# First-layer attention with key blocks 0-127, 128-255 and 256-271: the two 16x16 corners of four heads in one masked product

## The chip, the cores and the metric

One core of one Trainium2 chip runs the whole forward pass. The metric is the device time of one execution in microseconds (us).

## The reference

A two-layer decoder trunk in fp32: 16 meta tokens are put in front of 256 tokens (272 in all), model width 2048, 16 heads of 128, feed-forward width 8192. The first layer uses forgetting attention, the second stick-breaking attention; each is followed by a squared-ReLU MLP. The change touches the first layer's attention only:

```python
def forgetting_attention(q, k, v, cum_logf):
    for qs, qe in query_blocks(q.shape[1]):        # (0,16), (16,144), (144,272)
        s = jnp.einsum('bqhd,bkhd->bhqk', q[:, qs:qe], k[:, :qe]) * scale
        s = s + cum_logf[:, :, qs:qe, None] - cum_logf[:, :, None, :qe]
        s = jnp.where(k_pos[None, :] <= q_pos[:, None], s, -jnp.inf)
        p = jax.nn.softmax(s, axis=-1)
        outs.append(jnp.einsum('bhqk,bkhd->bqhd', p, v[:, :qe]))
```

So the queries 16-143 see the keys 0-143, and the queries 144-271 see the keys 0-271, each with the causal mask.

## The kernel before, in words

Activations lie feature-major: the 2048 features are 16 chunks of 128 partitions, with the tokens along the row. Every general product runs in `gemm_group`: 512 output features, 16 chunks of the contraction, four accumulators. Weights come by DMA as `raw` tiles; ScalarE rounds them to `whi` (line 197), VectorE puts the rest into `wlo` (line 198), and three products per chunk and output block (lines 220 to 222) give nearly fp32 precision. `raw`, `whi` and `wlo` each rotate through three buffers.

The first layer's attention runs over four groups of four heads. In a group the query, key and value projections are three calls of `gemm_group`, and the attention's own steps are spread between them:

- Scores: two products per head (line 365), for 128 queries against 144 keys and for 128 queries against 272 keys, in full fp32. The probabilities of a head lie in one tile `s` with 144 + 272 = 416 columns, queries on partitions. The 16 meta queries of the four heads go through one packed 64-row product (line 378) into `s0`.
- Transposes: to multiply by the values, the probabilities are turned with the keys on partitions. Per head that is three 128x128 transposes (lines 396 to 398) into `pp`, copied to `pp_sb`. The kernel before takes the key blocks as 0-15, 16-143, 144-271; the three transposes cover the last two.
- The meta block, keys 0-15: `packed` (line 316, on GpSimd) gathers 32 columns of each of the four heads into one 128-column tile `pk_sm`, once for each query block. Lines 403 to 405 transpose the two tiles and `s0` into `pm`, and ScalarE copies all of it to `pm_sb` (line 407).
- Values: after the value projection, `packed` gathers the first 32 values of the four heads (`pk_vm`); they are transposed (line 413), copied to `vm_sb` by ScalarE (line 415) and used at once for the meta queries (`pom`, line 419). GpSimd then copies the 16 meta rows of each head into its own slab of `vz` (line 417), a tile that is zero elsewhere, so that one 128-row product per head, line 426, adds the meta keys of that head alone for both query blocks.
- Output: per head the products of lines 426, 427 and 428 accumulate in `po`; `token_major` (line 307) supplies the transposed values in pairs of heads, and `put_split` (lines 321 and 322) writes the result as a rounded part and a rest for the output projection.

The code names an order, but a scheduler places the instructions of each engine: it works from its own model of their times and fills TensorE's queue with products of the next `gemm_group` between the attention's small steps. Each engine then runs its queue in order. PSUM tiles of the attention (`patt`) rotate through four buffers; `pm_sb` and `vm_sb` have one buffer each, `pk` has two.

SBUF tiles are laid pool by pool: `const`, which holds the masks and `vz`, comes ahead of the weight and activation pools.

Of the kernel before, what the change touches and what calls it, by code (L numbers as in the profile page):

```python
# [9 lines left out]
F32 = mybir.dt.float32  # L10
F32R = mybir.dt.float32r
AF = mybir.ActivationFunctionType
ALU = mybir.AluOpType
AX = mybir.AxisListType

P = 128
D = 2048
NC = D // P
M = 16
S = 256  # L20
T = M + S
# [11 lines left out]
def yoco_kernel(ctx: ExitStack, tc: tile.TileContext, hT_in, gains, b_f, w_f, w_qkv0, w_o0, w_up, w_dn,  # L33
                w_kv, w_q1, w_o1, outT):
    nc = tc.nc

    const = ctx.enter_context(tc.tile_pool(name="const", bufs=1))
# [21 lines left out]
    for _ in range(7):  # L59
# [41 lines left out]
                            pattern=[[M, 4], [1, M]], channel_multiplier=-1)  # L101
    nc.gpsimd.affine_select(out=maskC, in_=maskC, compare_op=ALU.is_ge, fill=-BIG, base=0,
                            pattern=[[-M, 4], [0, M]], channel_multiplier=1)

    pad = align.tile([P, 32], F32, name="pad")
    nc.gpsimd.memset(pad, 0.0)
# [205 lines left out]
    def packed(src, label):  # L312

        n = src.shape[2]
        t = att.tile([P, P], F32, tag="pk", name=f"pk_{label}")[:, :4 * n]
        nc.gpsimd.tensor_copy(t.rearrange("p (h t) -> p h t", h=4), src)
        return t

    def put_split(sp, h, nh, t, n, src):
        hi, lo = (x[:, h:h + nh, t - sp.t0:t - sp.t0 + n] for x in (sp.hi, sp.lo))  # L320
        nc.scalar.activation(hi, src, AF.Copy)
        nc.vector.tensor_tensor(out=lo, in0=src, in1=hi.bitcast(F32), op=ALU.subtract)


    vz = const.tile([P, 4, P], F32, name="vz")
    nc.gpsimd.memset(vz, 0.0)

    ao = Split("o0", 0)
    for g in range(4):
        qT = att.tile([P, 4, T], F32, tag="qT", bufs=4, name=f"qT0_{g}")  # L330
        kT = att.tile([P, 4, T], F32, tag="kT", bufs=1, name=f"kT0_{g}")
        vT = att.tile([P, 4, T], F32, tag="vT", bufs=1, name=f"vT0_{g}")

        def evac_q(m, acc, qT=qT):
            nc.vector.scalar_tensor_tensor(out=qT[:, m, :], in0=acc[0], scalar=-QSCALE, in1=box["rstd"],
                                           op0=ALU.mult, op1=ALU.mult)

        def evac_kv(m, acc, t):
            nc.vector.tensor_tensor(out=t[:, m, :], in0=acc[0], in1=box["rstd"], op=ALU.mult)

        if g == 0:
            gemm_group(w_qkv0[0], xa, 0, evac_q, after={kb: (lambda kb=kb: first_norm(kb)) for kb in range(4)}, load_x=load_x)
            forget_gates(box["rstd"])
        else:
            gemm_group(w_qkv0[3 * g], xa, 0, evac_q)
        fk = att.tile([P, 4, T], F32, tag="qT", bufs=4, name=f"fk_{g}")
        nc.scalar.dma_start(fk, f_dram[4 * g:4 * g + 4, :].unsqueeze(0).to_broadcast([P, 4, T]))
        s = att.tile([P, 4, 416], F32, tag="s", bufs=1, name=f"s_{g}")

        def decays(j):  # L350

            for i, (o, n) in enumerate(((0, 144), (144, T))):
                nc.vector.scalar_tensor_tensor(out=s[:, j, o:o + n], in0=fk[:, j, :n],
                                               scalar=fq_sb[:, i, 4 * g + j:4 * g + j + 1],
                                               in1=maskA[:, o:o + n], op0=ALU.subtract, op1=ALU.add)

        gemm_group(w_qkv0[3 * g + 1], xa, 0, lambda m, acc: evac_kv(m, acc, kT),
                   after={j: (lambda j=j: decays(j)) for j in range(4)})


        for j in range(4):
            h = 4 * g + j
            ps = patt.tile([P, 512], F32, tag="patt", name=f"ps_{h}")
            for q0, o, n in ((M, 0, 144), (M + P, 144, T)):
                nc.tensor.matmul(ps[:, o:o + n], qT[:, j, q0:q0 + P], kT[:, j, :n], start=True, stop=True)  # L365
            st = att.tile([P, 4], F32, tag="st", name=f"st_{h}")
            for i, (o, n) in enumerate(((0, 144), (144, T))):
                nc.vector.tensor_tensor_reduce(out=s[:, j, o:o + n], in0=ps[:, o:o + n], in1=s[:, j, o:o + n],
                                               scale=1.0, scalar=3.0e38, op0=ALU.add, op1=ALU.min,
                                               accum_out=st[:, i:i + 1])  # L370
                nc.scalar.activation(s[:, j, o:o + n], s[:, j, o:o + n], AF.Exp, bias=st[:, i:i + 1], scale=-1.0,
                                     accum_out=st[:, 2 + i:3 + i])
            nc.vector.reciprocal(st[:, 2:4], st[:, 2:4])
            for i, (o, n) in enumerate(((0, 144), (144, T))):
                nc.vector.tensor_scalar(s[:, j, o:o + n], s[:, j, o:o + n], st[:, 2 + i:3 + i], None, op0=ALU.mult)

        ps = patt.tile([P, 512], F32, tag="patt", name=f"ps0_{g}")
        nc.tensor.matmul(ps[:64, :P], packed(qT[:, :, :M], f"qm_{g}"), kT[:, :, :32], start=True, stop=True)
        s0 = att.tile([64, P], F32, tag="s0", name=f"s0_{g}")
        st = att.tile([P, 4], F32, tag="st", name=f"st0_{g}")  # L380
        nc.vector.scalar_tensor_tensor(out=s0.rearrange("p (h k) -> p h k", h=4), in0=fk[:64, :, :32],
                                       scalar=fqm_sb[:, g:g + 1], in1=maskM, op0=ALU.subtract, op1=ALU.add)
        nc.vector.tensor_tensor_reduce(out=s0, in0=ps[:64, :P], in1=s0, scale=1.0,
                                       scalar=3.0e38, op0=ALU.add, op1=ALU.min, accum_out=st[:64, 0:1])
        nc.scalar.activation(s0, s0, AF.Exp, bias=st[:64, 0:1], scale=-1.0, accum_out=st[:64, 1:2])
        nc.vector.reciprocal(st[:64, 1:2], st[:64, 1:2])
        nc.vector.tensor_scalar(s0, s0, st[:64, 1:2], None, op0=ALU.mult)


        pps = []  # L390
        for pr in range(2):
            pp_sb = att.tile([P, 2, 416], F32, tag="pp", bufs=3, name=f"pp_sb_{g}_{pr}")
            for i in range(2):
                j = 2 * pr + i
                pp = patt.tile([P, 512], F32, tag="patt", name=f"pp_{4 * g + j}")
                nc.tensor.transpose(pp[:, 0:P], s[:, j, M:144], ident)
                nc.tensor.transpose(pp[:, P:2 * P], s[:, j, 144 + M:144 + M + P], ident)
                nc.tensor.transpose(pp[:, 2 * P:3 * P], s[:, j, 144 + M + P:416], ident)
                nc.vector.tensor_copy(pp_sb[:, i, :3 * P], pp[:, :3 * P])
            pps.append(pp_sb)  # L400

        pm = patt.tile([P, 512], F32, tag="patt", name=f"pm_{g}")
        nc.tensor.transpose(pm[:, 0:P], packed(s[:, :, 0:32], f"sm0_{g}"), ident)
        nc.tensor.transpose(pm[:, P:2 * P], packed(s[:, :, 144:176], f"sm1_{g}"), ident)
        nc.tensor.transpose(pm[:, 2 * P:2 * P + 64], s0, ident[:64, :64])
        pm_sb = att.tile([P, 320], F32, tag="pm_sb", bufs=1, name=f"pm_sb_{g}")
        nc.scalar.copy(pm_sb, pm[:, :320])

        gemm_group(w_qkv0[3 * g + 2], xa, 0, lambda m, acc: evac_kv(m, acc, vT))


        pv = patt.tile([P, 512], F32, tag="patt", name=f"pvm_{g}")
        nc.tensor.transpose(pv[:, :P], packed(vT[:, :, 0:32], f"vm_{g}"), ident)
        vm_sb = att.tile([P, P], F32, tag="vm_sb", bufs=1, name=f"vm_sb_{g}")
        nc.scalar.copy(vm_sb, pv[:, :P])
        for j in range(4):
            nc.gpsimd.tensor_copy(vz[32 * j:32 * j + M, j, :], vm_sb[32 * j:32 * j + M, :])
        po = patt.tile([P, 512], F32, tag="patt", name=f"pom_{g}")
        nc.tensor.matmul(po[:, :64], vm_sb, pm_sb[:, 256:320], start=True, stop=True)
        put_split(ao, 4 * g, 4, 0, M, po[:, :64].rearrange("p (h q) -> p h q", h=4))  # L420
        for pr in range(2):
            v_sb = token_major(vT, pr, M, f"0_{g}_{pr}")
            po = patt.tile([P, 2, 256], F32, tag="patt", name=f"po0_{g}_{pr}")
            for i in range(2):
                j = 2 * pr + i
                nc.tensor.matmul(po[:, i, :], vz[:, j, :], pm_sb[:, :256], start=True, stop=False)  # L426
                nc.tensor.matmul(po[:, i, :], v_sb[:, i, 0, :], pps[pr][:, i, 0:2 * P], start=False, stop=False)  # L427
                nc.tensor.matmul(po[:, i, P:], v_sb[:, i, 1, :], pps[pr][:, i, 2 * P:3 * P], start=False, stop=True)  # L428
            put_split(ao, 4 * g + 2 * pr, 2, M, S, po)


# [73 lines left out]
    for g in range(4):  # L505
# [3 lines left out]
        q = qT1[g]  # L509
# [185 lines left out]
```

## Time and profile before

| | |
|---|---|
| median of three runs | 2360.81 us (2360.66 to 2361.17) |
| profiled execution | 2360.31 us, span 2358.6 us |
| TensorE busy | 2344.8 us, 99% |
| VectorE, ScalarE, GpSimd busy | 57%, 45%, 2% |
| granted TensorE clock, mean | 0.998 |
| read from HBM | 407.29 MB, 174 GB/s over the span |
| first layer's attention | about 40 to 360 us of the span |

A line of the trace names an engine, a source line, an operation, the tiles it writes and reads, and its shape. PE is TensorE's products, PEld its weight loads, DVE is VectorE, ACT ScalarE, POOL GpSimd, SP SyncE. The recorded duration of a product reaches beyond the start of the next one, because products are pipelined; what a product holds TensorE for is read from the distance between starts. A full fp32 product is recorded as two instructions.

### The profile page before, as it was taken

How to read it: one execution, taken by the hardware profiler on the slowest of the kernel's cores; microseconds unless marked ns; L12 is line 12 of the kernel's file. 1: busy time of each engine (PE TensorE's matmuls, PEld its weight loads, DVE VectorE, ACT ScalarE, POOL GpSimd, SP SyncE). 2: the span in 40 equal slices, each digit the busy share in tenths (PEclk: the TensorE clock that was granted, in tenths of full speed). 3: DMA queues.
4: the chain of work that ended last, by engine and by line, in shares of the span. 5: the costliest groups of instructions: out<-in, count | busy, mean ns of one | idle time of the engine just before them, and what ended most of it. 6: DMA issues, size and time to landing. Idle time of an engine off the chain costs nothing.

```text
span 2358.6 us, 39145 instructions
## 1 busy us (share of the span) xinstructions
PE 2344.8 (99%) x16512; PEld 2211.8 (94%) x16512; DVE 1343.1 (57%) x1916; ACT 1057.1 (45%) x1471; POOL 35.9 (2%) x64
## 2 busy tenths in 40 slices
PE   9999999999999999999999999999999999999998
PEld 9999999999999999999998999988888888888887
DVE  7565555655455455445566555566555655655665
ACT  5443344543344344344445444445543543543543
POOL 0000000000000000000000000000000000000000
PEclk9999999999999999999999999999999999999999
DMA  6444444554545455554545444445555555455453
GB/s 235 145 164 171 155 159 163 176 180 169 189 163 186 171 180 178 179 179 173 178 168 197 156 147 145 144 177 180 183 178 193 192 183 197 169 190 195 178 196 125
DMA packets 61039, 411.92 MB, mean 175 GB/s; under 512 B 7088, under 2 KB 10048, under 8 KB 12096
## 3 DMA queue, kind: packets, MB, share of 16 engines
q1 hardware_dynamic: 58976, 406.27, 48.5%
q8 instruction: 129, 2.11, 0.4%
q10 hardware_dynamic: 1888, 3.16, 0.4%
q14 instruction: 46, 0.38, 0.0%
HBM read 407.29 MB, written 2.11 MB: 174 GB/s over the span
## 4 chain that ended last, share of the span: by engine, by line
PE 99%; DVE 0%; ACT 0%; DMA 0%; issue 0%; DVEq 0%; SPq 0%; ACTq 0%
PE acc L217 25%; PE acc L220 19%; PE acc L221 19%; PE acc L222 19%; PE acc L218 13%; PE ps L365 0%; PE pza L542 0%; PE pv L307 0%; PE po L426 0%; PE po L427 0%; PE po L581 0%; PE po L582 0%; PE pzb L543 0%; PE po L428 0%; DMA g_sb<-gains 0%; ACT whi L197 0%
## 5 line engine op out<-in xcount | busy, mean ns | idle before, releaser
L198 DVE TENSOR_TENSOR wlo<-raw,whi 128x1024 fp32r<-128x1024 f32 (+1 forms) x771 | 932.5, 1220 | 761.5 <-ACT whi L197 758.2
L197 ACT ACTIVATE whi<-raw 128x1024 fp32r<-128x1024 f32 (+1 forms) x771 | 803.2, 1054 | 1072.4 <-PE acc L221 678.3
L217 PE MATMUL acc<-x_m,whi 128*128 128x512 f32 x1024 | 343.1, 394 | 0.5 <-DVE relu L235 0.5
L217 PE MATMUL acc<-x_u,whi 128*128 128x512 f32 x1008 | 337.9, 394 | 0.0
L220 PE MATMUL acc<-x_u,whi 128*128 128x272 f32 (+1 forms) x1040 | 297.7, 289 | 0.0
L221 PE MATMUL acc<-x_u,whi 128*128 128x272 f32 (+1 forms) x1040 | 294.8, 286 | 0.0
L220 PE MATMUL acc<-x_m,whi 128*128 128x272 f32 x1024 | 293.4, 289 | 0.0
L221 PE MATMUL acc<-x_m,whi 128*128 128x272 f32 x1024 | 290.4, 286 | 0.0
L222 PE MATMUL acc<-x_u,wlo 128*128 128x272 f32 (+1 forms) x1040 | 285.2, 284 | 0.0
L222 PE MATMUL acc<-x_m,wlo 128*128 128x272 f32 x1024 | 280.7, 284 | 0.0
L218 PE MATMUL acc<-x_m,wlo 128*128 128x256 f32 x1024 | 252.6, 282 | 0.0
L218 PE MATMUL acc<-x_u,wlo 128*128 128x256 f32 x1008 | 247.6, 281 | 0.0
L220 PE MATMUL acc<-x_a,whi 128*128 128x272 f32 x768 | 222.1, 294 | 0.7 <-ACT x_a L122 0.7
L221 PE MATMUL acc<-x_a,whi 128*128 128x272 f32 x768 | 221.0, 292 | 0.0
L217 PEld LDWEIGHTS acc<-x_m,whi 128*128 128x128 f32 x1024 | 185.0, 188 | 30.3 <-DVE relu L235 0.9
L222 PE MATMUL acc<-x_a,wlo 128*128 128x272 f32 x768 | 210.5, 287 | 0.0
L218 PEld LDWEIGHTS acc<-x_m,wlo 128*128 128x128 f32 x1024 | 192.3, 188 | 19.4 <-DVE wlo L198 4.6
L217 PEld LDWEIGHTS acc<-x_u,whi 128*128 128x128 f32 x1008 | 182.4, 188 | 29.7
L218 PEld LDWEIGHTS acc<-x_u,wlo 128*128 128x128 f32 x1008 | 189.3, 188 | 15.9 <-DVE wlo L198 1.6
L220 PEld LDWEIGHTS acc<-x_u,whi 128*128 128x128 f32 x1040 | 195.5, 188 | 0.2
L221 PEld LDWEIGHTS acc<-x_u,whi 128*128 128x128 f32 x1040 | 195.3, 188 | 0.1
L220 PEld LDWEIGHTS acc<-x_m,whi 128*128 128x128 f32 x1024 | 192.5, 188 | 0.0
(246 smaller groups left out, 3613.0 us busy)
## 6 DMA issues: line engine op xcount, KB each, us to landing
raw<-w_up SPq DMA_DIRECT2D x128, 1024.0 KB, 4.9
raw<-w_dn SPq DMA_DIRECT2D x128, 1024.0 KB, 4.9
raw<-w_qkv SPq DMA_DIRECT2D x45, 1024.0 KB, 4.8
raw<-w_o SPq DMA_DIRECT2D x32, 1024.0 KB, 4.8
raw<-w_kv SPq DMA_DIRECT2D x32, 1024.0 KB, 4.9
raw<-w_q SPq DMA_DIRECT2D x16, 1024.0 KB, 4.8
fk<-f_dram ACTq DMA_DIRECT2D x4, 544.0 KB, 5.2
raw<-w_qkv SPq DMA_DIRECT2D x4, 512.0 KB, 8.3
```

The lines of the kernel that those rows point to most:

```text
L197: on_act = nc.scalar.activation(hp, src, AF.Copy)
L198: on_dve = nc.vector.tensor_tensor(out=lp, in0=src, in1=hp.bitcast(F32), op=ALU.subtract)
L217: nc.tensor.matmul(accs[m], wh, sp.both[:, k], start=first, stop=False)
L218: nc.tensor.matmul(accs[m][:, :n], wl, hi, start=False, stop=last)
L220: nc.tensor.matmul(accs[m][:, :n], wh, hi, start=first, stop=False)
L221: nc.tensor.matmul(accs[m][:, :n], wh, lo, start=False, stop=False)
L222: nc.tensor.matmul(accs[m][:, :n], wl, hi, start=False, stop=last)
```

## The change

The key blocks become 0-127, 128-255 and 256-271. Now the three transposes per head cover the keys 0-127 for both query blocks and 128-255 for the second. What is left are two corners per head of 16 keys by 16 queries: the first query block's keys 128-143 and the second's keys 256-271. Because of the causal mask only the last 16 queries of each block see them.

`corners` gathers these columns of the four heads (two GpSimd copies into one 128-column tile), one transpose turns them, and VectorE multiplies the turned 16 columns, repeated eight times, with `maskD`, a block-diagonal mask of eight 16x16 blocks. The corner values are gathered by `corners` too, and transposed beside the meta values. One product per pair of heads then adds all four corners of the pair at the end of its accumulation group, into the last 16 columns of each of the four column blocks of `po`. `vz`, its four copies per group and the per-head products of line 426 go. ScalarE's copy of `pm` shrinks from 320 to 64 columns, and that of the values grows from 128 to 256.

```diff
+    maskD = const.tile([P, 8, M], F32, name="maskD")
+    nc.gpsimd.memset(maskD, 1.0)
+    nc.gpsimd.affine_select(out=maskD, in_=maskD, compare_op=ALU.is_ge, fill=0.0, base=0,
+                            pattern=[[-M, 8], [0, M]], channel_multiplier=1)
+    nc.gpsimd.affine_select(out=maskD, in_=maskD, compare_op=ALU.is_ge, fill=0.0, base=M - 1,
+                            pattern=[[M, 8], [0, M]], channel_multiplier=-1)
...
+    def corners(a, b, label):
+
+        t = att.tile([P, P], F32, tag="pk", name=f"pk_{label}")
+        for i, src in enumerate((a, b)):
+            nc.gpsimd.tensor_copy(t.rearrange("p (h c t) -> p h c t", h=4, c=2)[:, :, i, :], src)
+        return t
...
-    vz = const.tile([P, 4, P], F32, name="vz")
-    nc.gpsimd.memset(vz, 0.0)
...
-                nc.tensor.transpose(pp[:, 0:P], s[:, j, M:144], ident)
-                nc.tensor.transpose(pp[:, P:2 * P], s[:, j, 144 + M:144 + M + P], ident)
-                nc.tensor.transpose(pp[:, 2 * P:3 * P], s[:, j, 144 + M + P:416], ident)
+                nc.tensor.transpose(pp[:, 0:P], s[:, j, 0:P], ident)
+                nc.tensor.transpose(pp[:, P:2 * P], s[:, j, 144:144 + P], ident)
+                nc.tensor.transpose(pp[:, 2 * P:3 * P], s[:, j, 144 + P:144 + 2 * P], ident)
...
-        nc.tensor.transpose(pm[:, 0:P], packed(s[:, :, 0:32], f"sm0_{g}"), ident)
-        nc.tensor.transpose(pm[:, P:2 * P], packed(s[:, :, 144:176], f"sm1_{g}"), ident)
-        nc.tensor.transpose(pm[:, 2 * P:2 * P + 64], s0, ident[:64, :64])
-        pm_sb = att.tile([P, 320], F32, tag="pm_sb", bufs=1, name=f"pm_sb_{g}")
-        nc.scalar.copy(pm_sb, pm[:, :320])
+        nc.tensor.transpose(pm[:, 0:P], corners(s[:, :, P:144], s[:, :, 400:416], f"sm_{g}"), ident)
+        nc.tensor.transpose(pm[:, P:P + 64], s0, ident[:64, :64])
+        pm_sb = att.tile([P, 192], F32, tag="pm_sb", bufs=1, name=f"pm_sb_{g}")
+        nc.vector.tensor_tensor(out=pm_sb[:, :P].rearrange("p (b q) -> p b q", q=M), in1=maskD, op=ALU.mult,
+                                in0=pm[:, P - M:P].unsqueeze(1).to_broadcast([P, 8, M]))
+        nc.scalar.copy(pm_sb[:, P:], pm[:, P:P + 64])
...
-        vm_sb = att.tile([P, P], F32, tag="vm_sb", bufs=1, name=f"vm_sb_{g}")
-        nc.scalar.copy(vm_sb, pv[:, :P])
-        for j in range(4):
-            nc.gpsimd.tensor_copy(vz[32 * j:32 * j + M, j, :], vm_sb[32 * j:32 * j + M, :])
+        nc.tensor.transpose(pv[:, P:2 * P], corners(vT[:, :, P:144], vT[:, :, 256:T], f"vc_{g}"), ident)
+        vm_sb = att.tile([P, 2 * P], F32, tag="vm_sb", bufs=1, name=f"vm_sb_{g}")
+        nc.scalar.copy(vm_sb, pv[:, :2 * P])
...
-        nc.tensor.matmul(po[:, :64], vm_sb, pm_sb[:, 256:320], start=True, stop=True)
+        nc.tensor.matmul(po[:, :64], vm_sb[:, :P], pm_sb[:, P:], start=True, stop=True)
...
-            v_sb = token_major(vT, pr, M, f"0_{g}_{pr}")
+            v_sb = token_major(vT, pr, 0, f"0_{g}_{pr}")
...
-                nc.tensor.matmul(po[:, i, :], vz[:, j, :], pm_sb[:, :256], start=True, stop=False)
-                nc.tensor.matmul(po[:, i, :], v_sb[:, i, 0, :], pps[pr][:, i, 0:2 * P], start=False, stop=False)
-                nc.tensor.matmul(po[:, i, P:], v_sb[:, i, 1, :], pps[pr][:, i, 2 * P:3 * P], start=False, stop=True)
+                nc.tensor.matmul(po[:, i, :], v_sb[:, i, 0, :], pps[pr][:, i, 0:2 * P], start=i == 0, stop=False)
+                nc.tensor.matmul(po[:, i, P:], v_sb[:, i, 1, :], pps[pr][:, i, 2 * P:3 * P], start=False, stop=False)
+            nc.tensor.matmul(po.rearrange("p i (c q) -> p (i c) q", c=2)[:, :, P - M:], vm_sb[:, P:],
+                             pm_sb[:, 64 * pr:64 * pr + 64], start=False, stop=True)
```

More of the change, by code (lines that the diff above doesn't have):

```diff
@@ L413, in yoco_kernel @@
         nc.tensor.transpose(pv[:, :P], packed(vT[:, :, 0:32], f"vm_{g}"), ident)
-        vm_sb = att.tile([P, P], F32, tag="vm_sb", bufs=1, name=f"vm_sb_{g}")
-        nc.scalar.copy(vm_sb, pv[:, :P])
-        for j in range(4):
-            nc.gpsimd.tensor_copy(vz[32 * j:32 * j + M, j, :], vm_sb[32 * j:32 * j + M, :])
+        nc.tensor.transpose(pv[:, P:2 * P], corners(vT[:, :, P:144], vT[:, :, 256:T], f"vc_{g}"), ident)
+        vm_sb = att.tile([P, 2 * P], F32, tag="vm_sb", bufs=1, name=f"vm_sb_{g}")
+        nc.scalar.copy(vm_sb, pv[:, :2 * P])
         po = patt.tile([P, 512], F32, tag="patt", name=f"pom_{g}")
-        nc.tensor.matmul(po[:, :64], vm_sb, pm_sb[:, 256:320], start=True, stop=True)
+        nc.tensor.matmul(po[:, :64], vm_sb[:, :P], pm_sb[:, P:], start=True, stop=True)
         put_split(ao, 4 * g, 4, 0, M, po[:, :64].rearrange("p (h q) -> p h q", h=4))
         for pr in range(2):
-            v_sb = token_major(vT, pr, M, f"0_{g}_{pr}")
+            v_sb = token_major(vT, pr, 0, f"0_{g}_{pr}")
             po = patt.tile([P, 2, 256], F32, tag="patt", name=f"po0_{g}_{pr}")
             for i in range(2):
[L425 to L428, printed above, removed]
+                nc.tensor.matmul(po[:, i, :], v_sb[:, i, 0, :], pps[pr][:, i, 0:2 * P], start=i == 0, stop=False)
+                nc.tensor.matmul(po[:, i, P:], v_sb[:, i, 1, :], pps[pr][:, i, 2 * P:3 * P], start=False, stop=False)
+            nc.tensor.matmul(po.rearrange("p i (c q) -> p (i c) q", c=2)[:, :, P - M:], vm_sb[:, P:],
+                             pm_sb[:, 64 * pr:64 * pr + 64], start=False, stop=True)
             put_split(ao, 4 * g + 2 * pr, 2, M, S, po)
```

## The prediction

> **What bounds the kernel now.** I read the page first, then TensorE's own waits, then the busy time by stage, and last the single instructions around the products that change.
>
> The page's busy shares and the chain that ended last:
>
> ```profile
> PE 2344.8 (99%) x16512; PEld 2211.8 (94%) x16512; DVE 1343.1 (57%) x1916; ACT 1057.1 (45%) x1471; POOL 35.9 (2%) x64
> ...
> PE 99%; DVE 0%; ACT 0%; DMA 0%; issue 0%; DVEq 0%; SPq 0%; ACTq 0%
> ```
>
> The chain of waits ran on TensorE for 99% of the span. What TensorE waited for in the whole run (engine, line, releaser: us in total, times, longest):
>
> ```profile
> PE pr_fin L626 <- DVE fin L620: 1.3, 1, 1.3
> PE idle L60 <- DVE mean_w L56: 1.1, 1, 1.1
> PE pms_a L145 <- DVE ssq_a L140: 0.9, 1, 0.9
> PE acc L217 <- DVE qT L235: 0.9, 1, 0.9
> PE acc L220 <- ACT x_a L122: 0.7, 1, 0.7
> PE acc L217 <- DVE relu L235: 0.5, 1, 0.5
> ```
>
> None of these six waits is in the four head groups of the first attention. The busy time by stage says so again for that stretch (start:end, length, then each engine's busy us and instructions, clock, DMA share, GB/s):
>
> ```profile
> 40.00:360.00 320.00, 320.00 (x2492) 314.46 (x2492) 179.54 (x332) 127.83 (x195) 18.78 (x31) 1.00 0.45 159
> ```
>
> TensorE has no idle moment there, at full granted clock, while VectorE is 56% busy and ScalarE 40%. So each nanosecond that leaves TensorE's queue leaves the time, as long as no new wait takes its place. An edit on VectorE, ScalarE or GpSimd is worth nothing by itself.
>
> The changed places on TensorE, from the timeline of the first group (start us, us, instruction). A recorded duration overlaps the next one, so the cost of a product is the distance to the next start:
>
> ```profile
> 99.91 0.33 PE L419 MATMUL pom<-pm_sb,vm_sb 128*128 128x64 f32 x2
> 100.07 0.61 PE L307 MATMUL pv<-ident,vT 128*128 128x128 f32 x4
> 100.52 0.60 PE L426 MATMUL po<-pm_sb,vz 128*128 128x256 f32 x2
> 100.95 0.60 PE L307 MATMUL pv<-ident,vT 128*128 128x128 f32 x4
> ...
> 103.51 0.60 PE L426 MATMUL po<-pm_sb,vz 128*128 128x256 f32 x2
> 103.94 0.59 PE L427 MATMUL po<-pp_sb,v_sb 128*128 128x256 f32 x2
> 104.37 0.38 PE L428 MATMUL po<-pp_sb,v_sb 128*128 128x128 f32 x2
> 104.59 0.60 PE L426 MATMUL po<-pm_sb,vz 128*128 128x256 f32 x2
> ```
>
> An fp32 product is two instructions (x2). The padded meta product L426 holds TensorE for 0.43 us (103.51 to 103.94; 0.434 in the trace's unrounded starts), as much as the real 128x256 product L427 behind it. A 64-column product, L419, holds it for 0.165 us (99.911 to 100.076 unrounded), and the transpose behind it comes 6 ns late.
>
> **The change on TensorE.** Removed: one L426 per head, 16 in all: 16 x 0.434 = 6.94 us. Added: one corner product per pair of heads, 8 in all. It is 128 rows by 128 weight columns by 64 moving columns, the same form as L419, so I take 0.165 + 0.006 = 0.171 us each: 8 x 0.171 = 1.37 us. Two things could make it dearer. It writes four runs of 16 columns where L419 writes 64 in a row. The nearest stepped product is L583 of the second layer, which writes two runs of 16; it holds TensorE for some 0.48 us (133 + 203 ns to the next start, 94 more on the product before it and 55 on the transpose behind). But it has 64 rows, and so has the transpose L405, which costs about 0.40 us where a 128-row transpose costs 0.11: some 0.29 us belong to the 64 rows, and 0.19 are left. The other row is L594, one moving column, whose instructions settle at 112 ns each however little they move: two of them give 0.224. So the corner product lies between 0.11 (only its second half shows) and 0.224 us, and I take L419's value since its form is the same.
>
> One page speaks against that value. The Trainium skill, "TensorE: Matmul & The Clock Gate", section "LDWEIGHTS (loading the stationary operand)", gives a weight load 1/1.2 ns per column, thus 107 ns for 128 columns, whatever moves. By that rule, an estimate, two loads make 0.213 us per corner product, eight 1.71 us, and the gain would be 5.23 instead of 5.57 us. L419's 0.165 us disagrees and L594's 112 ns agrees, so both stay inside the range.
>
> Transposes: per group the old order has two for the packed probabilities and one for the packed values, the new one has one and two; each costs 0.11 us beside its neighbours, so this is nothing. The 64-row transpose L405 remains once per group, between general products as before. The 12 probability transposes and 8 value transposes keep their number and shape; only their columns move.
>
> Sum: 6.94 - 1.37 = 5.57 us less.
>
> **The change elsewhere, and its cover.** In the instruction order of the two built programs, everything outside the changed places is the same on all engines; SyncE's list and its DMAs are the same. Four places could make TensorE wait.
>
> (a) The new transpose of the packed corner values stands five general products behind that of the meta values, and waits for GpSimd's copies. Behind it in TensorE's queue are 24 general products. This stretch in the kernel before (timeline, all engines):
>
> ```profile
> 92.99 2.44 DVE L198 TENSOR_TENSOR wlo<-raw,whi 128x1024 fp32r<-128x1024 f32 x2
> 93.14 1.22 POOL L316 COPY pk_vm<-vT 128x128 f32<-128x128 f32 x1 [19.11 <-DVE vT L339]
> 96.17 0.27 PE L413 MATMUL pvm<-ident,pk_vm 128*128 128x128 f32 x1
> 97.20 0.25 ACT L415 COPY vm_sb<-pvm 128x128 f32<-128x128 f32 x1
> ```
>
> GpSimd is held up while VectorE runs a splitting pass: pk_vm takes 1.22 us beside L198, where the pk_sm copy of the same size takes 0.29 without it. The first corner copy starts at 94.36 and runs against the second L198, which ends at 95.43; the other then runs free, so both are done by about 95.9. At 1.22 us each they would be done at 96.80. TensorE asks at 96.17 + 0.11 + 5 x 0.125 = 96.90. So nothing is lost by either row; the tight one leaves 0.1 us, and I keep 0.2 us per group, 0.8 in all, for the range.
>
> (b) pom needs the longer vm_sb copy (256 columns, about 0.36 us between the rows of 128 at 0.25 and 320 at 0.43). It would end near 97.7, and pom comes at 99.9. The four vz copies (2.22 us, 97.51 to 99.73), which the first L426 needed by 100.52, are gone.
>
> (c) The new VectorE product with the mask waits for the transpose pm. VectorE's copy before it ends at 77.62 and pm is there at 77.4, so it runs at once for some 0.3 us (128x64 takes 0.22, 128x272 takes 0.44) and holds the next L198 back by 0.1 us. The splitting passes run ahead of TensorE: of ScalarE's 161.4 us idle before L197 in this stretch, 154.3 are waits for TensorE to free a buffer. Cost nothing.
>
> (d) The second pair's value transposes now follow the first pair's products, and ScalarE puts out the first pair before it copies them. From 100.07: 0.44 for transposes, 25 products (3.1), the pair (1.30 + 0.17), 0.44 for transposes: 105.5. ScalarE ends the first pair's put-out near 105.9 and the copy (0.59) near 106.5; the second pair's products come after 26 more products, at 108.8. Cover 2.3 us.
>
> At the start GpSimd trades a 0.52 us memset for a shorter one and two selects, and ends near 6.1 instead of 5.8 us. VectorE's L198 at 5.60 may be stretched; its output is used at 6.9. I take 0, and up to 0.4 us for the range.
>
> **The numbers.** The profiled execution took 2360.31 us, 1.7 outside its span; the sum gives 2354.74 for it. The median of the three runs is 2360.81, 0.50 higher, so I predict 2360.81 - 5.57 = 2355.2. A measurement of this kernel can tell about 0.2% (4.7 us) from no change.
>
> **Rivals.** *Gain within 0.2%.* The corner product costs 0.224 and (a) and the start come out at their bad ends: 6.94 - 1.79 - 0.8 - 0.4 = 3.95 less, 2356.9. For it: L594 and the thin 0.1 us. Against: the form of L419, and GpSimd's last copy running free. It needs two of three together to fall below 4.7. Chance 0.15.
>
> *Slower.* The constants shrink: vz's 2048 bytes per partition go and maskD's 512 come, so every buffer laid behind them moves by 1536 bytes. If TensorE's reads of weights or activations care where a buffer lies, all of some 16,000 general products change. It decides from 0.35 ns per product, which eats the gain; 0.65 ns makes it 0.2% slower, and 1 ns gives 2371. Against it: in the profile products on three activation buffers and three rotating weight buffers have the same distance to the next start (L220 126.4, L221 125.0, L222 122.0 ns on x_o; 126.4 to 126.5, 125.0 and 122.0 on x_m and x_u). Chance 0.05.
>
> *The change doesn't do what it says.* The built program has the 16 padded products out and 8 corner products in, so this has no chance of its own.
>
> **Chances and range.** My forecast has 0.80, all of it over 0.2% faster (5.15 at a corner of 0.224 alone is still 0.22%). The low end is the corner at 0.11 (gain 6.06, 2354.7) less 0.3 for the spread of the runs; the high end is the first rival's, 2356.9, which takes most of its chance in. So 0.80 faster, 0.15 same, 0.05 slower.
>
> **What would show it.** Right: no L426 rows with vz, eight corner products at 0.16 to 0.18 us to the next start, TensorE still without idle time from 40 to 360 us, and groups shorter by 1.39 us each. Wrong: TensorE idle in front of the corner values' transpose with GpSimd as releaser; corner products at 0.2 us or more; general products at another distance than 125 ns on average.

## The result and the profile after

The median went from 2360.78 to 2355.44 us (twelve runs each), 5.34 us less; the ratio is 0.9978, with a 95% interval from 0.9971 to 0.9985. The forecast was 2355.2 us, in a range from 2354.4 to 2356.9. The profiled execution took 2355.27 us, 5.04 less than the one of before.

The page of the changed kernel, busy shares and the chain that ended last:

```profile
PE 2339.7 (99%) x16496; PEld 2207.5 (94%) x16496; DVE 1343.7 (57%) x1920; ACT 1056.2 (45%) x1471; POOL 33.4 (1%) x58
...
PE 99%; DVE 0%; ACT 0%; DMA 0%; issue 0%; DVEq 0%; SPq 0%; ACTq 0%
```

TensorE has 16 instructions fewer (32 of the padded products out, 16 of the corner products in) and 5.1 us less busy time. It is still the whole chain. Its waits in the whole run, and the attention's stretch in the table of busy time by stage:

```profile
PE pr_fin L639 <- DVE fin L633: 1.3, 1, 1.3
PE idle L60 <- DVE mean_w L56: 1.1, 1, 1.1
PE acc L225 <- DVE qT L243: 0.9, 1, 0.9
PE pms_a L153 <- DVE ssq_a L148: 0.9, 1, 0.9
PE acc L228 <- ACT x_a L130: 0.8, 1, 0.8
PE acc L225 <- DVE relu L243: 0.5, 1, 0.5
```

```profile
40.00:360.00 320.00, 320.00 (x2518) 315.65 (x2518) 181.84 (x338) 129.36 (x197) 15.63 (x23) 1.00 0.45 159
```

These are the same six waits as before, and none is new. So the records show the gain as pure queue length; as recorded durations overlap by some 0.16 us, a wait shorter than that would not show in them. The places on TensorE in the first group, from the timeline (start us, us, instruction); L432 is the meta product, L438 and L439 the real ones, L440 the corner product and L315 the value transposes:

```profile
104.86 0.38 PE L439 MATMUL po<-pp_sb,v_sb 128*128 128x128 f32 x2
105.08 0.33 PE L440 MATMUL po<-pm_sb,vm_sb 128*128 128x64 f32 x2
105.25 0.61 PE L315 MATMUL pv<-ident,vT 128*128 128x128 f32 x4
...
110.03 0.38 PE L439 MATMUL po<-pp_sb,v_sb 128*128 128x128 f32 x2
110.25 0.33 PE L440 MATMUL po<-pm_sb,vm_sb 128*128 128x64 f32 x2
110.40 0.37 PE L230 MATMUL acc<-x_a,wlo 128*128 128x272 f32 x1
110.61 0.29 PE L228 MATMUL acc<-x_a,whi 128*128 128x272 f32 x1
```

In unrounded starts the corner product of the first pair takes 58 + 112 ns to the transpose, and 10 more are lost behind it (119 ns where transposes take 109): 0.180 us. That of the second pair takes 59 + 84 ns to the general product, which then takes 211 instead of 125. It does so behind a 128-column product without a corner too: in e1 below, L439's second instruction takes 31 ns to the general product, and that one 209. With the corner, L439's second instruction takes 111 ns, 80 more, so the corner costs 80 + 59 + 84 = 0.223 us.

How long a group is can be read from GpSimd, which makes one copy of the meta values per group:

```profile
93.17 1.22 POOL L324 COPY pk_vm<-vT 128x128 f32<-128x128 f32 x1 [19.14 <-DVE vT L350]
94.34 1.40 POOL L331 COPY pk_vc<-vT 128x64 f32<-128x64 f32 x2
...
174.49 1.22 POOL L324 COPY pk_vm<-vT 128x128 f32<-128x128 f32 x1 [19.14 <-DVE vT L350]
```

The distance from one pk_vm to the next is 81.31 us; before it was 82.62 (93.14 to 175.76). It repeats to 5 ns over the three distances of an execution, and it is the finest measure here: 1.309 us per group, 5.24 for four. The prediction said 1.39. What separates 5.24 from the 5.04 of the two profiled executions lies outside the groups.

### The profile page after: what moved, and what is told of

Read it like the earlier page. It is cut to its first block, busy times and chain, and to the rows that moved or that the text cites. A ratio compares the mean times of both kernels' runs of the same rounds, so it can differ in the third digit from the quotient of the medians.

```text
span 2353.6 us, 39103 instructions
## 1 busy us (share of the span) xinstructions
PE 2339.7 (99%) x16496; PEld 2207.5 (94%) x16496; DVE 1343.7 (57%) x1920; ACT 1056.2 (45%) x1471; POOL 33.4 (1%) x58
## 4 chain that ended last, share of the span: by engine, by line
PE 99%; DVE 0%; ACT 0%; DMA 0%; issue 0%; DVEq 0%; SPq 0%; ACTq 0%
PE acc L225 25%; PE acc L228 19%; PE acc L229 19%; PE acc L230 19%; PE acc L226 13%; PE ps L376 0%; PE pza L555 0%; PE pv L315 0%; PE po L438 0%; PE po L594 0%; PE pzb L556 0%; PE po L595 0%; PE po L439 0%; DMA g_sb<-gains 0%; ACT whi L205 0%; PE po L596 0%
## 5 line engine op out<-in xcount | busy, mean ns | idle before, releaser
L228 PE MATMUL acc<-x_u,whi 128*128 128x272 f32 (+1 forms) x1040 | 297.7, 289 | 0.0
L229 PE MATMUL acc<-x_u,whi 128*128 128x272 f32 (+1 forms) x1040 | 294.8, 286 | 0.0
L228 PE MATMUL acc<-x_m,whi 128*128 128x272 f32 x1024 | 293.4, 289 | 0.0
L229 PE MATMUL acc<-x_m,whi 128*128 128x272 f32 x1024 | 290.4, 286 | 0.0
L230 PE MATMUL acc<-x_u,wlo 128*128 128x272 f32 (+1 forms) x1040 | 285.2, 284 | 0.0
L230 PE MATMUL acc<-x_m,wlo 128*128 128x272 f32 x1024 | 280.7, 284 | 0.0
L228 PE MATMUL acc<-x_a,whi 128*128 128x272 f32 x768 | 222.6, 294 | 0.8 <-ACT x_a L130 0.8
L229 PE MATMUL acc<-x_a,whi 128*128 128x272 f32 x768 | 220.2, 291 | 0.0
L230 PE MATMUL acc<-x_a,wlo 128*128 128x272 f32 x768 | 211.2, 288 | 0.0
L228 PEld LDWEIGHTS acc<-x_u,whi 128*128 128x128 f32 x1040 | 195.5, 188 | 0.2
L229 PEld LDWEIGHTS acc<-x_u,whi 128*128 128x128 f32 x1040 | 195.1, 188 | 0.1
L228 PEld LDWEIGHTS acc<-x_m,whi 128*128 128x128 f32 x1024 | 192.5, 188 | 0.0
```

Of the source, the lines that this page charges most:

```text
L228: nc.tensor.matmul(accs[m][:, :n], wh, hi, start=first, stop=False)
L229: nc.tensor.matmul(accs[m][:, :n], wh, lo, start=False, stop=False)
L230: nc.tensor.matmul(accs[m][:, :n], wl, hi, start=False, stop=last)
```

## The experiments

Each kernel is compared by that distance, the middle one of the three, from unrounded starts. Of e1, e2, e4, e5, e7, e8, e10 and e11 there is one execution each.

| kernel | group, us | against |
|---|---|---|
| before | 82.621 | |
| changed | 81.312 | before: -1.309 |
| e1, no corner products | 80.920 | changed: -0.392 |
| e2, before without padded products | 80.900 | before: -1.721 |
| e4, corner writes in a row | 81.314 | changed: +0.002 |
| e5, corner of 128 columns | 81.347 | changed: +0.035 |
| e10, corner one place earlier | 81.346 | changed: +0.034 |
| e8, transpose of 128 rows | 81.039 | changed: -0.273 |
| e11, GpSimd late | 81.307 | changed: -0.005 |
| e7, mask built later | 81.313 | changed: +0.001 |
| e13, changed again | 81.312 | changed: 0.000 |
| e9, both 64-wide steps of the first layer 128 wide | 80.660 | changed: -0.652 |
| e12, e9 and the second layer's 64-row steps | 80.660 | changed: -0.652 |

### The two terms of the sum

e1 and e2 take one term each.

```diff
 # e1, on the changed kernel
-                ... pps[pr][:, i, 2 * P:3 * P], start=False, stop=False)
-            nc.tensor.matmul(po.rearrange("p i (c q) -> p (i c) q", c=2)[:, :, P - M:], vm_sb[:, P:],
-                             pm_sb[:, 64 * pr:64 * pr + 64], start=False, stop=True)
+                ... pps[pr][:, i, 2 * P:3 * P], start=False, stop=i == 1)
 # e2, on the kernel before
-                nc.tensor.matmul(po[:, i, :], vz[:, j, :], pm_sb[:, :256], start=True, stop=False)
-                ... pps[pr][:, i, 0:2 * P], start=False, stop=False)
+                ... pps[pr][:, i, 0:2 * P], start=True, stop=False)
```

> The changed kernel without its eight corner products (the four 16x16 corners are missing from the result); every other instruction and its order stay. Theory A (the price of a corner product depends on what stands behind it, 0.180 us before a transpose and 0.223 us before a general product, as the changed kernel's trace has it): the span falls by 4 x (0.180 + 0.223) = 1.61 us against the changed kernel's, 0.40 us per head group. Theory B (the price is that of the meta product, 0.171 us, and what the gain lacks lies elsewhere): 1.37 us, 0.34 per group.

> The kernel before without its 16 padded meta products (the keys 0-15 are missing for all queries but the meta ones); the GpSimd copies into the padded tile stay. Theory A (TensorE is the bound, so each product is worth its distance to the next start): a group is 4 x 0.434 = 1.74 us shorter, 82.62 to 80.88, and the span 6.94 us. Theory B (part of the products only filled time in which the next step was not ready): less, under 1.6 us per group, with idle time of TensorE in its place.

The padded products are worth 1.721 us per group, 6.88 in all, where the sum had 6.94: theory A, each is worth its distance to the next start. In e2 the scheduler also moved the second pair's value transposes behind the first pair's products, as in the changed kernel, so e2 measures the removal together with this new order.

The two corner products of a group cost 0.392 us: between the theories, but much nearer to A (0.403) than to B (0.342). The second pair's handover from the last fp32 step to the general products, in e1:

```profile
109.99 0.38 PE L439 MATMUL po<-pp_sb,v_sb 128*128 128x128 f32 x2
110.13 0.37 PE L230 MATMUL acc<-x_a,wlo 128*128 128x272 f32 x1
110.34 0.28 PE L228 MATMUL acc<-x_a,whi 128*128 128x272 f32 x1
```

From L439 to L228 it takes 0.35 us, and 0.58 in the changed kernel (110.03 to 110.61).

The whole spans fell by less than four groups give: 1.38 us in e1 and 6.64 in e2, against 1.57 and 6.88. In these single executions the start (up to GpSimd's first copy of queries) and the stretch behind the second layer's first pk_kc copy took 0.20 and 0.22 us longer, taken together, which makes up most of the difference.

1.721 - 0.392 is 1.329, and 1.309 was measured; 0.02 us per group stay unassigned. The same 0.02 lies between e2 (80.900) and e1 (80.920), which differ on TensorE only in the packed transposes, a term that the prediction put at nothing. No single place in the rows holds it, so where it lies stays open.

### What sets the price of a 64-column product

e4, e5 and e10 change only the corner product and keep the order of all other instructions on every engine.

```diff
 # e4
-            nc.tensor.matmul(po.rearrange("p i (c q) -> p (i c) q", c=2)[:, :, P - M:], vm_sb[:, P:],
+            nc.tensor.matmul(po[:, 1, 2 * P - 64:], vm_sb[:, P:],
 # e5: the whole product becomes
+            nc.tensor.matmul(po[:, 1, P:], vm_sb[:, P:],
+                             pm_sb[:, :P], start=False, stop=True)
 # e10: ahead of the last product of the pair, in place of behind it
 ...
+                if i == 1:
+                    nc.tensor.matmul(po.rearrange("p i (c q) -> p (i c) q", c=2)[:, :, P - M:], vm_sb[:, P:],
+                                     pm_sb[:, 64 * pr:64 * pr + 64], start=False, stop=False)
```

> The changed kernel with the corner product writing 64 columns in a row in place of four runs of 16 (the corners land in the wrong columns). Theory A (the weight load behind a short product sets its price): no change, under 0.02 us per group. Theory C (the stepped write costs): both corner products of a group fall to 0.171 us, 0.06 us per group.

The stepped write costs nothing that can be seen (2 ns per group), so theory C falls.

> The changed kernel with a corner product of 128 moving columns in place of 64, written in a row (the result is wrong by that). Theory A (the weight loads set the price of so short a product, so that 64 columns are hardly cheaper than 128): 0.221 us each, like the other 128-column products: 0.04 us more before the transposes, nothing more before the general products, 0.04 us per group. Theory D (the columns set the price): twice the price of 64, 0.36 and 0.45 us, 0.40 us more per group.

Twice the columns cost 0.035 us per group more, as theory A said (0.04); D (0.40) falls. The timeline of e5, first pair and second pair:

```profile
105.84 0.39 PE L440 MATMUL po<-pm_sb,vm_sb 128*128 128x128 f32 x2
106.06 0.60 PE L315 MATMUL pv<-ident,vT 128*128 128x128 f32 x4
...
111.04 0.39 PE L440 MATMUL po<-pm_sb,vm_sb 128*128 128x128 f32 x2
111.19 0.37 PE L230 MATMUL acc<-x_a,wlo 128*128 128x272 f32 x1
111.40 0.29 PE L228 MATMUL acc<-x_a,whi 128*128 128x272 f32 x1
```

The second pair's handover, 111.04 to 111.40, takes the same 0.36 us as 110.25 to 110.61 in the changed kernel, with twice the columns. So the 64 columns are not what this product takes its time for.

> The changed kernel with the corner product one place earlier, ahead of the last 128-column product of its pair, so that the same fp32 product stands behind it in both pairs. Theory A (the price depends on what stands behind): 0.18 us in both pairs, the second pair gains 0.04 us per group, 0.17 us in all. Theory B (the price is the product's own): no change in either pair.

Neither theory held as it was put: the second pair gained nothing, and the first one became dearer, 0.224 us by its rows instead of 0.180; the group is 0.034 us longer. The timeline of e10 says why (L442 is the last 128-column product of the pair):

```profile
105.50 0.33 PE L440 MATMUL po<-pm_sb,vm_sb 128*128 128x64 f32 x2
105.67 0.44 PE L442 MATMUL po<-pp_sb,v_sb 128*128 128x128 f32 x2
105.94 0.60 PE L315 MATMUL pv<-ident,vT 128*128 128x128 f32 x4
```

L442 takes 165 + 111 ns behind the corner where it takes 109 + 112 elsewhere. Ahead of an fp32 product the corner is paid as 56 + 112 ns of its own and 56 on the product behind it, 0.224 us in all; ahead of a general product it came to 0.223. Only a transpose behind it pays 10 instead of 56. So the price does depend on the follower, as theory A had it, but the cheap follower is the transpose alone and not any fp32 step: theory A had the wrong class. L419, the row on which the prediction built, has a transpose behind it.

0.224 is two times the 112 ns at which L594's one-column instructions stood in the trace of before. e5 has the same 112 ns at 128 moving columns, so 1, 64 and 128 columns all show it. This fits the Trainium skill, "TensorE: Matmul & The Clock Gate", section "LDWEIGHTS (loading the stationary operand)", whose rule of 1/1.2 ns per weight column makes 107 ns for 128 of them, an estimate, whatever moves. That the weight load is the cause is inferred from this; no run changed the load alone. Why a transpose behind the corner pays so little no run here isolates; its recorded weight load is the shorter one in the traces (about 140 ns against 190), and that is as far as they go.

### The price of 64 rows

The prediction took 0.29 us off the second layer's stepped product L583 as the price of its 64 rows. e8 tests that on the changed kernel's 64-row transpose:

```diff
+    s0_all = const.tile([P, P], F32, name="s0_all")
+    nc.gpsimd.memset(s0_all, 0.0)
+    s0 = s0_all[:64]
...
-        s0 = att.tile([64, P], F32, tag="s0", name=f"s0_{g}")
...
-        nc.tensor.transpose(pm[:, P:P + 64], s0, ident[:64, :64])
+        nc.tensor.transpose(pm[:, P:2 * P], s0_all, ident)
```

> The changed kernel with the meta queries' probabilities in a 128-row tile whose upper 64 rows are zero, so that their transpose takes 128 rows in place of 64. It tests the price that the prediction took off the 64-row product of the second layer. Theory A (a change between 64 and 128 rows costs TensorE 0.29 us around the product): 0.29 us less per group, 1.16 us in all. Theory B (the time there is a wait for the tile): no change.

0.273 us per group came back: theory A. In the timeline, the changed kernel first, then e8, with the general products beside the transposes:

```profile
77.29 0.37 PE L230 MATMUL acc<-x_a,wlo 128*128 128x272 f32 x1
77.59 0.27 PE L416 MATMUL pm<-ident,s 64*128 64x64 f32 x1
77.79 0.39 PE L228 MATMUL acc<-x_a,whi 128*128 128x272 f32 x1
78.02 0.29 PE L229 MATMUL acc<-x_a,whi 128*128 128x272 f32 x1
```

```profile
77.41 0.37 PE L230 MATMUL acc<-x_a,wlo 128*128 128x272 f32 x1
77.62 0.27 PE L419 MATMUL pm<-ident,s_all 128*128 128x128 f32 x1
77.65 0.37 PE L228 MATMUL acc<-x_a,whi 128*128 128x272 f32 x1
77.86 0.29 PE L229 MATMUL acc<-x_a,whi 128*128 128x272 f32 x1
```

From the general product ahead to the second one behind it is 0.73 us around a 64-row transpose and 0.45 around a 128-row one, though the latter moves twice the columns and writes four times the values.

### The rival with GpSimd, and the start

```diff
 # e11: eight more copies ahead of the corner values' two (again is 8 there and 0 elsewhere)
-        for i, src in enumerate((a, b)):
+        for i, src in [(0, a)] * again + [(0, a), (1, b)]:
```

> The changed kernel with eight more GpSimd copies ahead of the corner values' two, so that the transpose's operand comes some 2 us later. The scheduler, which knows them, puts that transpose further back in TensorE's queue. Theory A (the gain doesn't hang on the place of the transpose): a group takes the same 81.32 us to 0.1. Rival (GpSimd's chain is the tight spot of the change): TensorE waits in front of the transpose for GpSimd, up to 0.5 us per group.

GpSimd's corner copies took 4.64 us instead of 1.40, the transpose came at 100.66 instead of 96.94 us, and the group stayed at 81.307 us. The scheduler had moved the transpose and all that hangs on it back, and general products filled the place. So the tight spot that the prediction kept 0.8 us for is elastic as long as the scheduler knows the delay. A delay that it doesn't know was not tried.

For e7 the mask was built from ones that VectorE writes in the first group, with the two GpSimd selects behind them.

> The changed kernel with the corner mask built in the first group (ones from VectorE, then the two GpSimd selects) in place of the start. The changed kernel reached GpSimd's first copy of queries 0.15 us later than the kernel before (38.34 against 38.19 us). Theory E (GpSimd's two more selects at the start hold VectorE and ScalarE up): it comes back to 38.19. Theory F (the start differs from execution to execution, by when the first transfers land): it stays anywhere between 38.1 and 38.5, not tied to the mask.

GpSimd's first copy came at 38.26 us, nearly as early as before; read alone, that is theory E. But the changed kernel itself, profiled again as e13, came at 38.56 instead of 38.34, and the others with the mask at the start lie anywhere from 38.27 (e12) over 38.43 to 38.48 (e11, e8, e1) to between 38.8 and 39.1 (e9, e10, e4, e5). The start moves by itself by more than the 0.15 us in question. The three kernels without the early mask (before, e2, e7) are all at 38.30 or earlier, so a small price of the mask is not excluded; it stays open.

### A version that beats both

The 64-row price led to two more kernels. In e9 the meta queries' scores also take 128 weight columns (the 64 queries twice). In e12 the second layer's packed corner of 16 keys per head becomes 32 keys, 240 to 271, in 128 rows, with the extra 16 masked out.

```diff
 # e9, beside e8's edit
+        for i in range(2):
+            nc.gpsimd.tensor_copy(qm[:, i], qT[:, :, :M])
...
+        nc.tensor.matmul(ps[:, :P], qm.rearrange("p i h t -> p (i h t)"), kT[:, :, :32], start=True, stop=True)
 # e12, beside e9's edits; the same form for vT, nones and the tiles zc, ec, vc_sb
+    maskC = const.tile([P, 4, M], F32, name="maskC")          # selects with base M and -M, steps of 32
...
+        nc.tensor.matmul(pz[:, :64], packed(kT[:, :, 240:T], f"kc_{g}"), q[:, :, 240:S], start=True, stop=True)
...
+        nc.tensor.matmul(pt[:, :64], ntri, ec, start=True, stop=True)
```

> The changed kernel with 128 rows and 128 weight columns in the two 64-wide steps of the first layer's attention: the meta queries' probabilities are transposed from a 128-row tile (0.27 us per group, as measured) and the meta queries' scores take 128 weight columns, the 64 queries twice, in place of 64. Theory A (64-wide steps cost TensorE extra around them: 93 + 160 + 202 + 103 = 0.56 us for the scores in the changed kernel's trace, against 0.22 for a 128-wide product of 128 columns): 0.27 + 0.33 = 0.60 us per group, a group at 80.71 us, and 2.4 us in all: 2353.0. Theory B (only the transpose gains): 1.1 us, 2354.3.

> The kernel of e9 with the second layer's packed corner steps widened as well: 32 keys per head, 240 to 271, in 128 rows in place of 16 keys in 64, the other 16 masked out. Theory A (by the distances in the changed kernel's trace: 0.46 to 0.22 us for the scores, 0.81 to 0.45 for the two sums, 0.49 and 0.54 to 0.18 and 0.22 for the two value products): 1.2 us per group of the second layer, 4.8 us in all over e9, 2348.2. Theory B (part of it was cover for waits in the corner chain, which then show): 2 to 4 us over e9.

> The changed kernel itself once more, as the measure for the two others on the same chip, and for the start: groups of 81.31 us, 2355.4 us in all. If the start differs from execution to execution, GpSimd's first copy of queries comes anywhere between 38.2 and 39.1 us; if the mask at the start sets it, at 38.34 again.

On one chip, with five runs of e9 and of e12, eleven of the changed kernel and fifteen of the one before: e9 2352.67 us, ratio to the kernel before 0.9968 (0.9956 to 0.9981); e12 2347.61 us, 0.9946 (0.9934 to 0.9959); the changed kernel again 2355.12 us, 0.9978 (0.9969 to 0.9987); the kernel before 2360.45. Theory A holds in both: e9's group is 80.66 us (80.71 expected; 0.38 of the gain are e9 less e8, the scores of 64 weight columns, where 0.33 was expected), and the second layer's group, from one pk_kc copy to the next, went from 58.58 to 57.31 us, 1.27 (1.2 expected). The busy time of e12 by stage, for both layers' attention:

```profile
40.00:360.00 320.00, 320.00 (x2539) 317.74 (x2538) 183.74 (x341) 129.18 (x200) 18.04 (x26) 1.00 0.46 162
1300.00:1540.00 240.00, 240.00 (x1829) 235.02 (x1828) 138.87 (x189) 116.51 (x144) 9.79 (x8) 1.00 0.44 154
```

TensorE is without recorded idle time in both stretches, so this gain, too, is queue length. Widening gained more than the change under study: 7.5 us beyond the changed kernel by the medians of that chip.

## Why the prediction was right, point by point

- **TensorE as the bound.** Held: no new wait, no idle time from 40 to 360 us, and the padded products worth their distance to the next start (6.88 of 6.94 us, e2).
- **The corner product.** This term was mis-sized: 0.171 us each by L419, against 0.180 and 0.223 in the trace and 0.196 on average by e1. Eight of them cost 1.57 us instead of 1.37. The form was the same as L419's, but for one product of each group's two the follower was not, and the follower decides. The range had this end (0.224); the choice between the ends failed. By the prediction's own signs, 0.2 us or more was to show it wrong, and four of the eight products reached that; the mere distance to the next start (0.170 and 0.143 us) would have hidden it. The estimate by the Trainium skill's load time came nearer: eight products at 1.71 us are 0.14 too much, where 1.37 are 0.20 too little. That its gain of 5.23 us meets the four groups' 5.24 is luck, as the sum's other terms were off by as much the other way.
- **The stepped write.** The bound of 0.19 us from L583 less the price of its 64 rows was sound in both parts: the step costs nothing that can be seen (e4), and a step of 64 rows, tested on the transpose, costs 0.273 (e8; 0.29 was taken). L583 itself was not changed alone.
- **The covers.** (a) GpSimd was done at 95.74 us (95.9 said) and the transpose came at 96.94 (96.90 said). (b) The longer copy took 0.374 us (0.36) and ended at 97.6, with pom at 100.0. (c) The product with the mask took 0.292 us (0.3). (d) The second pair came at 108.95 (108.8). No wait of TensorE is recorded at any of them.
- **The rivals.** Of the gain within 0.2% only the dear corner came true, and that for half of the products; the waits didn't. The rival of moved buffers didn't show: the general products stand at the same distances as before (L228 126.5, L229 125.0, L230 122.0 ns on x_m, as L220 to L222 had), with all buffers 1536 bytes lower.
- **The median.** It fell by 5.34 us where the groups gave 5.24: the shortfall of 0.33 against 5.57 is 0.20 from the corner, 0.06 from the padded products and about 0.08 unassigned in the groups. The remaining 0.10 of the median lies outside the groups and is within the spread of the runs, which were 2354.83 to 2355.94 us; that it brought the median nearer to the forecast is luck.

## What to carry to other kernels

Where one engine is the whole chain, cost an instruction by the distance between starts, in the order in which the built program will have it: a price read from a row holds for its follower as well as for its form. Here an fp32 product of 64 moving columns was no cheaper than one of 128 (0.224 us) unless a transpose stood behind it (0.180), so count products, not columns. A step of 64 rows or 64 weight columns between 128-wide ones can cost more than its padded 128-wide form (0.27 us for a transpose, 0.38 for a product of scores); padding it is worth a try.

## What the runs showed that was not expected

A 64-row transpose costs 0.27 us more than a 128-row one of twice the columns, since it holds TensorE longer itself (204 ns to the next start against 30) and lengthens its neighbours on both sides (302 and 229 ns beside it, 209 and 210 beside the wide one). The same widening in the second layer gave 5.1 us of 2352.

A product that writes four runs of 16 columns to PSUM is as fast as one that writes 64 in a row (81.312 us per group against 81.314 in e4). The Trainium skill, "SBUF — State Buffer", section "Door 1: The DMA port swizzle (why `[64,N]` ≈ `[32,N]`)", says that any non-contiguous access of PSUM slows products down significantly; for runs of 16 fp32 values in this product the trace disagrees. As twice the columns hardly changed its time (e5), a smaller slowdown of the write itself could hide here, and in a longer product no run tried it.
